# The decayed queries and keys of an HGRN2 level in one tile, scaled and split in one step of 512 columns

## The chip, the cores and the metric

The kernel runs on one core of a Trainium2 chip. The metric is the device time of one execution in microseconds (us). The program is built once; a scheduler in the build decides the order of the instructions on each engine, and on the chip each engine works through its own list in that order, waiting on semaphores where an operand isn't ready. The engines are named PE (TensorE), ACT (ScalarE), DVE (VectorE), POOL (GpSimd) and SP (SyncE, which here issues the weight DMAs).

## The reference

One step of a decoder trunk with two layers, for a prompt of 256 tokens and 8 single sample tokens; the width is 2048. Layer 0 mixes tokens by sliding-window attention and layer 1 by HGRN2, a gated linear recurrence with 12 heads of 128. Both layers have four memory heads, a SiLU gate, one output projection and a LayerNorm. The part that the change touches is the recurrence of the prompt, cut here to what matters:

```python
fg = lb + (1 - lb) * sigmoid(f)          # decay of each token and channel
q, k, v = silu(q), 1 - fg, iv
g_cum = cumsum(log(fg), axis=time)
decay[t, s] = exp(g_cum[t] - g_cum[s])   # s <= t, else 0
scores[t, s] = sum_k q[t, k] * decay[t, s, k] * k[s, k]
o = scores @ v + (q * exp(g_cum)) @ state
o = o * rsqrt(mean(o ** 2) + eps) * norm_w
```

## The kernel before

**The weight stream.** The kernel is a stream of units. A unit is a tile of weights (or of a cache) of 128 x 2048 float32, loaded by the SP queue. `prep` of `Stream` splits it into two float16 parts: the rounded value, hi, on ACT (L97) and the remainder, lo, on DVE (L98); four raw tiles and four split tiles are in flight. The unit's function then multiplies. `passes` (L302 to L305) writes each product as three float16 matmuls: hi by hi (L303), hi by lo (L304), lo by hi (L305). A projection (`proj`, L307) is 16 chunks of three matmuls with 264 columns, 256 prompt tokens and 8 sample tokens.

**Layer 1.** The 12 heads go in six pairs. For each head there are units for the gate f (`f_unit`), the values (`hv_unit`), the queries (`hq_unit`) and the samples' states (`state_unit`). Once the second query of a pair is there, the recurrence of the pair's prompt part is put on as a side (`hg_side`), a generator of which one step runs behind each unit. The last pair's side falls into the time of the memory queries (mq), the samples' memory caches (ck, matmuls mss; cv, matmuls mso) and the gate projections of layer 1 (matmuls g). Behind these come the 16 units of the output projection.

**The side of a pair.** The causal decay is applied level by level, h = 1, 2, 4 up to 64. At a level the tokens form blocks of 2h; the queries of the second half of a block meet the keys of its first half. `qa` (float32) holds the queries times their decay so far, `K`, the prompt's 256 columns of `kk`, the keys. `prepare(h)` splits the first halves of K into `ksp` and the second halves of qa into `qsp` (hi on ACT, L1075, lo on DVE, L1076), and multiplies the same elements by the decays of the level (L1078 for the queries, L1081 for the keys). Each of these steps covers 256 columns: two heads of 128 elements. `products(h)` makes 12 matmuls of 64 columns (hs; stationary ksp, moving qsp) into half of a PSUM bank, and `keep(h)` copies the scores of the level into `st` by a mask on DVE. The four `ksp` buffers are zeroed once, so that the second halves add nothing.

**The end of a side.** `pk` and `kn` turn the decayed keys, `pu` (L1156, float32) multiplies them with the values, `s` and `hpo` (L1167 to L1169) give the outputs, `osb` and `osq` hold the outputs and their squares, `rms` (L1180) sums the squares, and Ln (L1181) and Exp (L1183) make the root of it, for both heads. DVE then scales and gates the result (L1186, L728, L730). The tiles hd, rms, hs and msc (the scores of the memory heads) take turns in two PSUM banks under the tag "sc", so a tile there waits until the second last one before it has been read.

**The order.** Nothing in the source fixes the order between the units and a side's steps beyond the order in which the code is written; the scheduler places the instructions by their dependencies and its own estimates. A change of one tile's shape can therefore move instructions far from it.

Of the kernel before, what the change touches and what calls it, by code (L numbers as in the profile page):

```python
# [35 lines left out]
SA = 8.0  # L36
SP = 1024.0
SK = 2048.0
# [8 lines left out]
LEVELS = (1, 2, 4, 8, 16, 32, 64)  # L47
# [87 lines left out]
def trunk_kernel(  # L135
# [32 lines left out]
    nc = tc.nc  # L168
# [113 lines left out]
    side = deque()  # L282
# [683 lines left out]
    H = {}  # L966

    def open_l1():
        l0.close()
        p1 = l1.enter_context(tc.tile_pool(name="p1", bufs=1))  # L970
        H["p"] = p1
        H["mask"] = p1.tile([P, NMASK], I32, name="mask_t")
        nc.gpsimd.dma_start(H["mask"], mask_d)
        H["sel"] = p1.tile([2 * TS, TS, P], F16, name="sel_t")
        nc.gpsimd.dma_start(H["sel"], sel_d)
        H["ksp"] = [p1.tile([P, 2, 2, TP], F16, name=f"ksp{i}") for i in range(4)]
        for t in H["ksp"]:
            nc.gpsimd.memset(t, 0.0)

    def f_unit(h):  # L980
        def fn(hl):
            if h == 0:
                drain()
                open_l1()
            p1 = H["p"]
            pt = proj(hl, xhl, T, f"f{h}")
            i = h % 2
            if i == 0:
                cur["fg"] = p1.tile([P, 2, T], F32, tag="fg", name=f"fg{h}", bufs=2)
                cur["kk"] = p1.tile([P, 2, T], F32, tag="kk", name=f"kk{h}", bufs=2)  # L990
                cur["ks8"] = p1.tile([P, 2, TS], F32, tag="ks8", name=f"ks8{h}", bufs=2)
            fg, kk, ks8 = cur["fg"][:, i], cur["kk"][:, i], cur["ks8"][:, i]
            th = p1.tile([P, T], F32, tag="th", name=f"th{h}", bufs=2)
            nc.scalar.activation(th, pt, AF.Tanh, scale=0.5 * CP)
            half, mid, half_k, nhalf_k = (hl_lb[:, k, h : h + 1] for k in range(4))
            nc.scalar.activation(fg, th, AF.Identity, bias=mid, scale=half)
            nc.scalar.activation(kk, th, AF.Identity, bias=half_k, scale=nhalf_k)
            nc.vector.tensor_scalar_mul(ks8, kk[:, TP:T], 1.0 / (SA * SK))

        return fn  # L1000

# [2 lines left out]
    def hq_unit(h):  # L1004
        def fn(hl):
            p1 = H["p"]
            pt = proj(hl, xhl, T, f"hq{h}")
            if h % 2 == 0:
                cur["q"] = p1.tile([P, 2, T], F32, tag="hq", name=f"hqs{h}", bufs=2)
            silu2(cur["q"][:, h % 2], pt)  # L1010
            if h % 2 == 1:
                side.append(hg_side(h // 2, cur["q"], cur["vn"], cur["fg"], cur["kk"]))

        return fn

# [35 lines left out]

    osb = {}

    def hg_side(pi, q, vn, fg, kk):
        p1, mask = H["p"], H["mask"]
        h0 = 2 * pi
        K = kk[:, :, :TP]
        Q = q[:, :, :TP]
        st = p1.tile([P, 4, P], F32, tag="st", name=f"st{pi}", bufs=1)
        qa = p1.tile([P, 2, TP], F32, tag="qa", name=f"qa{pi}", bufs=1)  # L1060
# [3 lines left out]
        parts = {}  # L1064

        def prepare(h):
            nonlocal f, off
            n = TP // (2 * h)
            k4 = K.rearrange("p i (n s t) -> p i n s t", s=2, t=h)
            q4 = qa.rearrange("p i (n s t) -> p i n s t", s=2, t=h)  # L1070
            ksp = H["ksp"][LEVELS.index(h) % 4].rearrange("p l i (n s t) -> p l i n s t", s=2, t=h)
            qsp = p1.tile([P, 2, 2, P], F16, tag="qsp", name=f"qsp{pi}_{h}", bufs=4)
            q5 = qsp.rearrange("p l i (n t) -> p l i n t", t=h)
            for hi, lo, src in ((ksp[:, 0, :, :, 0], ksp[:, 1, :, :, 0], k4[:, :, :, 0]), (q5[:, 0], q5[:, 1], q4[:, :, :, 1])):
                nc.scalar.activation(hi, src, AF.Copy)  # L1075
                nc.vector.tensor_tensor(lo, src, hi, op=ALU.subtract)  # L1076
            parts[h] = qsp
            nc.vector.tensor_tensor(  # L1078
                q4[:, :, :, 1], q4[:, :, :, 1], f[:, :, :, 0].unsqueeze(3).to_broadcast([P, 2, n, h]), op=ALU.mult
            )  # L1080
            nc.vector.tensor_tensor(  # L1081
                k4[:, :, :, 0], k4[:, :, :, 0], f[:, :, :, 1].unsqueeze(3).to_broadcast([P, 2, n, h]), op=ALU.mult
            )
            nxt = prod[:, off : off + 2 * n].rearrange("p (i n) -> p i n", i=2)
            if h < 64:
                nc.vector.tensor_tensor(nxt, f[:, :, :, 0], f[:, :, :, 1], op=ALU.mult)
            else:
                nc.vector.scalar_tensor_tensor(nxt, f[:, :, :, 0], 1.0 / SK, f[:, :, :, 1], op0=ALU.mult, op1=ALU.mult)
            off += 2 * n
            if h < 64:  # L1090
                f = nxt.rearrange("p i (n s) -> p i n s", s=2)
            return nxt
# [101 lines left out]
    def state_unit(h):  # L1194
        def fn(hl):
            p1 = H["p"]
            pi, i = h // 2, h % 2
            raw = stream.raw[state_at[h]][:, : TS * P]
            R = raw.rearrange("p (b v) -> p b v", b=TS)
            v = hl[:, :, : TS * P].rearrange("p s (b v) -> p s b v", b=TS)  # L1200
            vr, fgs, ks8 = cur["vr"][:, i], cur["fg"][:, i, TP:T], cur["ks8"][:, i]
            qs, ks, vts = (cur[n][:, i, TP:T] for n in ("q", "kk", "vt"))
# [7 lines left out]
            nc.scalar.activation(qfh[:, :, 0], qf, AF.Copy)  # L1210
# [24 lines left out]
        return fn  # L1235
# [189 lines left out]
```

## Time and profile before

| what | value |
|---|---|
| three runs | 910.62, 910.87, 908.19 us; median 910.62 us |
| the profiled execution: time, span | 909.74 us, 908.0 us |
| mean granted TensorE clock | 0.994 |
| POOL busy | 34.5 us (4%) |
| HBM | 179.80 MB read, 17.22 MB written, 217 GB/s over the span |
| hi of a weight tile, 128x2048, ACT L97 | 1906 ns, 146 of them |
| lo of a weight tile, 128x2048, DVE L98 | 2289 ns, 146 of them |
| a copy of 128x264 on ACT, L997 (kk from th) | 597 ns, 12 of them |
| the six pairs on the time axis | the first hs matmul starts at 465.0 us, the last at 762.9 us |

An engine's busy time is the sum of its instructions' durations. In a timeline, a matmul's row shows its duration with the time in the pipeline; what the engine spends on one is the distance to the next one's start. "Waits" are idle time of an engine in front of an instruction, put down to what ended last before it started. A row of groups gives the line, the engine, the operation, its tiles and shapes, the count, then busy us and mean ns of one, and then the idle time in front of it with its releaser.

### The profile page before, as it was taken

What the parts mean: (1) busy time and instruction counts of PE and PEld (TensorE: products, weight loads), DVE (VectorE), ACT (ScalarE), POOL (GpSimd) and SP (SyncE); (2) the same over time, 40 slices, a digit from 0 to 9 for tenths busy, and PEclk for the clock granted to TensorE, in tenths of its full rate; (3) what the DMA queues carried; (4) which work ended last, traced back from release to release, by engine and by line L of the source; (5) the groups of instructions that cost most, each with busy time, mean ns of one, the idle gap of its engine ahead of it and who ended that gap; (6) DMA issues with size and microseconds to landing.
All of it is one profiled execution on the core that took longest, in us unless ns stands there. A gap on an engine that the chain in (4) does not pass through costs nothing.

```text
span 908.0 us, 21927 instructions
## 1 busy us (share of the span) xinstructions
PE 893.3 (98%) x9281; PEld 764.0 (84%) x9281; DVE 704.2 (78%) x1302; ACT 581.8 (64%) x1000; POOL 34.5 (4%) x65
## 2 busy tenths in 40 slices
PE   9999999999999999999999999999999999899996
PEld 6888889678888888866888888888888888788996
DVE  6879887669886666696697897978888899778736
ACT  6767777567654533576766777676778576948415
POOL 1100010000000000002000000000000000000000
PEclk9999999999999999999999999999999999899999
DMA  9998565567685555555384555726454778566302
GB/s 349 379 369 312 189 242 210 198 210 266 252 318 191 210 204 187 192 203 196 125 310 147 196 183 179 292 100 260 160 208 170 258 267 310 180 251 239 134 1 97
DMA packets 37806, 198.44 MB, mean 219 GB/s; under 512 B 4556, under 2 KB 10733, under 8 KB 17485
## 3 DMA queue, kind: packets, MB, share of 16 engines
q1 hardware_dynamic: 33024, 181.55, 55.4%
q0 software_dynamic: 4640, 15.44, 4.6%
q8 instruction: 72, 1.18, 0.5%
q14 instruction: 26, 0.21, 0.1%
q10 hardware_dynamic: 44, 0.07, 0.1%
HBM read 179.80 MB, written 17.22 MB: 217 GB/s over the span
## 4 chain that ended last, share of the span: by engine, by line
PE 85%; DVE 5%; ACT 4%; DMA 4%; issue 1%; SPq 0%; ACTq 0%; DVEq 0%
PE g L305 6%; PE g L303 6%; PE g L304 6%; PE o L303 5%; PE o L305 5%; PE o L304 5%; PE q L303 2%; PE hv L304 2%; PE hv L303 2%; PE q L304 2%; PE hv L305 2%; PE q L305 2%; PE f L305 2%; PE f L303 2%; PE f L304 2%; ACT hl L97 2%
## 5 line engine op out<-in xcount | busy, mean ns | idle before, releaser
L98 DVE SCALAR_TENSOR_TENSOR hl<-raw,hl 128x2048 f16<-128x2048 f32 (+2 forms) x168 | 358.4, 2137 | 84.4 <-ACT hl L97 83.7
L97 ACT ACTIVATE hl<-raw 128x2048 f16<-128x2048 f32 (+2 forms) x168 | 298.8, 1784 | 87.3 <-PE o L305 45.3
L305 PEld LDWEIGHTS <-hl 128*128 128x128 f16 (+2 forms) x2048 | 197.5, 98 | 32.1 <-DVE hl L98 2.3
L303 PEld LDWEIGHTS <-hl 128*128 128x128 f16 (+2 forms) x2048 | 197.5, 98 | 31.6 <-ACT xhl L249 1.2
L304 PEld LDWEIGHTS <-hl 128*128 128x128 f16 (+2 forms) x2048 | 197.4, 98 | 30.8 <-issue 2.2
L305 PE MATMUL g<-xhl,hl 128*128 128x264 f16 x512 | 142.1, 278 | 1.8 <-DVE hl L98 1.8
L303 PE MATMUL g<-xhl,hl 128*128 128x264 f16 x512 | 142.1, 278 | 0.0
L304 PE MATMUL g<-xhl,hl 128*128 128x264 f16 x512 | 142.1, 278 | 0.0
L303 PE MATMUL o<-mix,hl 128*128 128x264 f16 x384 | 105.5, 276 | 0.7 <-DVE xres L747 0.7
L305 PE MATMUL o<-mix,hl 128*128 128x264 f16 x384 | 105.9, 276 | 0.0
L304 PE MATMUL o<-mix,hl 128*128 128x264 f16 x384 | 105.8, 276 | 0.0
L303 PE MATMUL q<-xhl,hl 128*128 128x264 f16 x192 | 53.0, 276 | 0.5 <-DVE kst L251 0.5
L303 PE MATMUL f<-xhl,hl 128*128 128x264 f16 x192 | 52.9, 276 | 0.4 <-DVE mvhl L251 0.4
L303 PE MATMUL hq<-xhl,hl 128*128 128x264 f16 x192 | 53.1, 276 | 0.0
L304 PE MATMUL hq<-xhl,hl 128*128 128x264 f16 x192 | 53.0, 276 | 0.0
L305 PE MATMUL hq<-xhl,hl 128*128 128x264 f16 x192 | 53.0, 276 | 0.0
L303 PE MATMUL hv<-xhl,hl 128*128 128x264 f16 x192 | 53.0, 276 | 0.0
L304 PE MATMUL hv<-xhl,hl 128*128 128x264 f16 x192 | 53.0, 276 | 0.0
L305 PE MATMUL hv<-xhl,hl 128*128 128x264 f16 x192 | 53.0, 276 | 0.0
L304 PE MATMUL q<-xhl,hl 128*128 128x264 f16 x192 | 53.0, 276 | 0.0
L305 PE MATMUL q<-xhl,hl 128*128 128x264 f16 x192 | 53.0, 276 | 0.0
L305 PE MATMUL f<-xhl,hl 128*128 128x264 f16 x192 | 53.0, 276 | 0.0
(337 smaller groups left out, 1868.4 us busy)
## 6 DMA issues: line engine op xcount, KB each, us to landing
raw<-in_w_in SPq DMA_DIRECT2D x88, 1024.0 KB, 5.5
raw<-in_w_o SPq DMA_DIRECT2D x32, 1024.0 KB, 4.9
raw<-in_w_mk SPq DMA_DIRECT2D x8, 1024.0 KB, 4.9
raw<-in_w_mv SPq DMA_DIRECT2D x8, 1024.0 KB, 4.9
raw<-in_c_mk SPq DMA_DIRECT2D x8, 1024.0 KB, 5.3
raw<-in_c_mv SPq DMA_DIRECT2D x8, 1024.0 KB, 4.8
raw<-in_state SPq DMA_DIRECT2D x12, 512.0 KB, 4.4
out_ss<-raw POOLq DMA_DIRECT2D x12, 512.0 KB, 2.9
```

What stands on the lines that cost most here:

```text
L97: hi = self.nc.scalar.activation(hl[:, 0, s], raw[:, s], AF.Copy, scale=scale)
L98: lo = self.nc.vector.scalar_tensor_tensor(hl[:, 1, s], raw[:, s], scale, hl[:, 0, s], op0=ALU.mult, op1=ALU.subtract)
L303: mm(out, lhs(0), rhs(0), start=start, stop=False)
L304: mm(out, lhs(0), rhs(1), start=False, stop=False)
L305: return mm(out, lhs(1), rhs(0), start=False, stop=stop)
```

## The change

The float32 queries `qa` and keys `K` become the two halves of one tile `qk32`, 128 x 2 (q, k) x 2 heads x 256. `f_unit` writes the prompt's keys into it, and the sample tokens' keys, 8 columns, into a `kk` of their own by an ACT instruction of its own. The four `ksp` tiles and the rotating `qsp` tiles become four tiles with hi and lo of both. `halves_of(t, h)` describes, in one access pattern, the queries' second halves and the keys' first halves of a level. `prepare(h)` makes one hi copy, one lo subtraction and one multiplication of 512 columns, where each was two of 256. The moving operand of hs is read in place, in runs of h elements with gaps of h, where qsp had it without gaps. Only the keys' half of the float16 tiles is zeroed.

```diff
-        H["ksp"] = [p1.tile([P, 2, 2, TP], F16, name=f"ksp{i}") for i in range(4)]
-        for t in H["ksp"]:
-            nc.gpsimd.memset(t, 0.0)
+        H["qk"] = [p1.tile([P, 2, 2, 2, TP], F16, name=f"qk16_{i}") for i in range(4)]
+        for t in H["qk"]:
+            nc.gpsimd.memset(t[:, :, 1], 0.0)
...
+                cur["qk"] = p1.tile([P, 2, 2, TP], F32, tag="qk32", name=f"qk32_{h}", bufs=2)
+                cur["kk"] = p1.tile([P, 2, TS], F32, tag="kk", name=f"kk{h}", bufs=2)
...
-            nc.scalar.activation(kk, th, AF.Identity, bias=half_k, scale=nhalf_k)
-            nc.vector.tensor_scalar_mul(ks8, kk[:, TP:T], 1.0 / (SA * SK))
+            nc.scalar.activation(cur["qk"][:, 1, i], th[:, :TP], AF.Identity, bias=half_k, scale=nhalf_k)
+            nc.scalar.activation(kk, th[:, TP:T], AF.Identity, bias=half_k, scale=nhalf_k)
+            nc.vector.tensor_scalar_mul(ks8, kk, 1.0 / (SA * SK))
...
+    def halves_of(t, h):
+        a, n = t[:, 0, 0, h : h + 1], TP // (2 * h)
+        inner = [[TP, 2], [2, n]] if h == 1 else [[2 * h, 2 * n], [1, h]]
+        return bass.AP(tensor=a.tensor, offset=a.offset, ap=[list(a.ap[0]), [2 * TP - h, 2], *inner])
...
-            for hi, lo, src in ((ksp[:, 0, :, :, 0], ksp[:, 1, :, :, 0], k4[:, :, :, 0]), (q5[:, 0], q5[:, 1], q4[:, :, :, 1])):
-                nc.scalar.activation(hi, src, AF.Copy)
-                nc.vector.tensor_tensor(lo, src, hi, op=ALU.subtract)
-            parts[h] = qsp
-            nc.vector.tensor_tensor(
-                q4[:, :, :, 1], q4[:, :, :, 1], f[:, :, :, 0].unsqueeze(3).to_broadcast([P, 2, n, h]), op=ALU.mult
-            )
-            nc.vector.tensor_tensor(
-                k4[:, :, :, 0], k4[:, :, :, 0], f[:, :, :, 1].unsqueeze(3).to_broadcast([P, 2, n, h]), op=ALU.mult
-            )
+            src = halves_of(qk, h)
+            hi, lo = (halves_of(H["qk"][LEVELS.index(h) % 4][:, s], h) for s in range(2))
+            nc.scalar.activation(hi, src, AF.Copy)
+            nc.vector.tensor_tensor(lo, src, hi, op=ALU.subtract)
+            by = f.rearrange("p i n s -> p s i n")
+            if h > 1:
+                by = by.rearrange("p s i n -> p s (i n)").unsqueeze(3).to_broadcast([P, 2, 2 * n, h])
+            nc.vector.tensor_tensor(src, src, by, op=ALU.mult)
...
         def products(h, sc):
-            qsp, ksp = parts.pop(h), H["ksp"][LEVELS.index(h) % 4]
+            t = H["qk"][LEVELS.index(h) % 4]
+            q5 = t[:, :, 0].rearrange("p l i (c n s t) -> p l i c n s t", c=2, s=2, t=h)
...
-                    lambda s: ksp[:, s, i, c * P : (c + 1) * P],
-                    lambda s: qsp[:, s, i, c * 64 : (c + 1) * 64],
+                    lambda s: t[:, s, 1, i, c * P : (c + 1) * P],
+                    lambda s: q5[:, s, i, c, :, 1],
```

In the built programs DVE has 1102 rows where it had 1190, ACT 772 where it had 796; PE has as many instructions as before, and SP issues the same DMAs in the same order. ACT's table loads are 20 where they were 16. In the changed program the lines of the RMS block stand one line higher (Ln at L1180, Exp at L1182, rms at L1179). The scheduler gives other places to many instructions; the following three are those of the last two pairs. Numbers behind names tell buffers apart.

The first place is ACT in the RMS block of the fifth pair, among the memory queries. Before (osq: the squares; rms: their sums; qsp and ksp: splits of the last pair's first levels; hl: hi of a weight tile):

```order
L97 ACTIVATE hl_10199<-raw_10035 128x2048
L1181 ACT_TABLE_LOAD
L1181 ACTIVATE osq_10047<-rms_10107,eps_rms 128x264
L1075 ACTIVATE qsp_1_10182<-qa_10174 128x256
L1181 ACTIVATE osq_10049<-rms_10110,eps_rms 128x264
L1183 ACT_TABLE_LOAD
L1183 ACTIVATE osq_10047<-osq_10047 128x264
L1183 ACTIVATE osq_10049<-osq_10049 128x264
L1075 ACTIVATE qsp_2_10191<-qa_10174 128x256
```

The same place in the changed program (qk_1: the split of both at the second level):

```order
L97 ACTIVATE hl_10150<-raw_9910 128x2048
L1180 ACT_TABLE_LOAD
L1180 ACTIVATE osq_9920<-rms_9980,eps_rms 128x264
L1182 ACT_TABLE_LOAD
L1182 ACTIVATE osq_9920<-osq_9920 128x264
L1180 ACT_TABLE_LOAD
L1180 ACTIVATE osq_9922<-rms_9983,eps_rms 128x264
L1182 ACT_TABLE_LOAD
L1182 ACTIVATE osq_9922<-osq_9922 128x264
L1076 ACTIVATE qk_1_5654<-qk_10_9343 128x2x128x2
```

The first head's Exp has moved ahead of the second head's Ln, with a table load on each side of it. On PE, the 12 hs of the last pair's first level now stand directly behind its hd, where 13 matmuls of mq stood between them.

The second place is ACT in the RMS block of the last pair. Before (sil: a gate's SiLU; msphl: the split of the samples' memory probabilities):

```order
L1171 ACTIVATE osb_9827<-hpo_10750 128x2x256
L1175 ACTIVATE osq_10758<-osb_9827 128x264
L1175 ACTIVATE osq_10760<-osb_9827 128x264
L97 ACTIVATE hl_10959<-raw_10693 128x2048
L733 ACTIVATE sil_11013<-g_10964 128x264
L249 ACTIVATE msphl_10815<-mback_10812 128x64
L1181 ACT_TABLE_LOAD
L1181 ACTIVATE osq_10758<-rms_10818,eps_rms 128x264
L1181 ACTIVATE osq_10760<-rms_10821,eps_rms 128x264
L1183 ACT_TABLE_LOAD
L1183 ACTIVATE osq_10758<-osq_10758 128x264
L1183 ACTIVATE osq_10760<-osq_10760 128x264
```

And in the changed program:

```order
L1170 ACTIVATE osb_9700<-hpo_10594 128x2x256
L1174 ACTIVATE osq_10602<-osb_9700 128x264
L1174 ACTIVATE osq_10604<-osb_9700 128x264
L1180 ACT_TABLE_LOAD
L1180 ACTIVATE osq_10602<-rms_10662,eps_rms 128x264
L1182 ACT_TABLE_LOAD
L1182 ACTIVATE osq_10602<-osq_10602 128x264
L1180 ACT_TABLE_LOAD
L1180 ACTIVATE osq_10604<-rms_10665,eps_rms 128x264
L249 ACTIVATE msphl_10659<-mback_10656 128x64
L1182 ACT_TABLE_LOAD
L1182 ACTIVATE osq_10604<-osq_10604 128x264
```

Here too the first Exp has moved ahead of the second Ln; and the hi of a weight tile and a SiLU that stood between the squares and the first Ln have moved to ahead of `s` and behind the block.

The third place is PE at the end of the last pair. Before, this is how the block around rms began (g: a gate projection; mback: the samples' probabilities, turned back):

```order
L677 MATMUL mback_10812<-ident,mrows_10804 128x32 x2
L305 LDWEIGHTS hl_10905
L305 MATMUL g_11094<-xhl,hl_10905 128x264
L303 LDWEIGHTS hl_10905
L303 MATMUL g_11094<-xhl,hl_10905 128x264
L304 LDWEIGHTS hl_10905
L304 MATMUL g_11094<-xhl,hl_10905 128x264
L1180 MATMUL rms_10818<-osq_10758,ones_rms 128x264
```

In the changed program the block from pu to the first msc reads:

```order
L1155 MATMUL pu_10523<-vn_9499,kn_10484 128x128 x4
L666 MATMUL mrow_10645<-ident,mst_10643 32x128 x2
L1168 MATMUL hpo_10594<-qk_10_9343,s_10528 128x128
L1166 MATMUL hpo_10594<-st_10046,vn_9499 128x128
L1167 MATMUL hpo_10594<-st_10046,vn_9499 128x128
L1168 MATMUL hpo_10594<-qk_10_9343,s_10528 128x128
L1179 MATMUL rms_10662<-osq_10602,ones_rms 128x264
L1179 MATMUL rms_10665<-osq_10604,ones_rms 128x264
L677 MATMUL mback_10656<-ident,mrows_10648 128x32 x2
L303 LDWEIGHTS mqhl
L303 MATMUL msc_10732<-mkhl,mqhl 128x256
```

Before, 80 matmuls of two gate projections (32 of g_10964 and 48 of g_11094) stood between pu and the last mso. Now all matmuls of the gate projections that are ready stand ahead of pu, two of hpo stand there as well, and between pu and the next gate projection PE has only the pair's own chain, msc, mso and mpt.

More of the change, by code (lines that the diff above doesn't have):

```diff
@@ L989, in fn @@
                 cur["fg"] = p1.tile([P, 2, T], F32, tag="fg", name=f"fg{h}", bufs=2)
-                cur["kk"] = p1.tile([P, 2, T], F32, tag="kk", name=f"kk{h}", bufs=2)
+                cur["qk"] = p1.tile([P, 2, 2, TP], F32, tag="qk32", name=f"qk32_{h}", bufs=2)
+                cur["kk"] = p1.tile([P, 2, TS], F32, tag="kk", name=f"kk{h}", bufs=2)
                 cur["ks8"] = p1.tile([P, 2, TS], F32, tag="ks8", name=f"ks8{h}", bufs=2)
@@ L1011, in fn @@
             if h % 2 == 1:
-                side.append(hg_side(h // 2, cur["q"], cur["vn"], cur["fg"], cur["kk"]))
+                side.append(hg_side(h // 2, cur["q"], cur["vn"], cur["fg"], cur["qk"]))
         return fn
@@ L1052, in trunk_kernel, with hg_side @@
     osb = {}
-    def hg_side(pi, q, vn, fg, kk):
+    def halves_of(t, h):
+        a, n = t[:, 0, 0, h : h + 1], TP // (2 * h)
+        inner = [[TP, 2], [2, n]] if h == 1 else [[2 * h, 2 * n], [1, h]]
+        return bass.AP(tensor=a.tensor, offset=a.offset, ap=[list(a.ap[0]), [2 * TP - h, 2], *inner])
+    def hg_side(pi, q, vn, fg, qk):
         p1, mask = H["p"], H["mask"]
         h0 = 2 * pi
-        K = kk[:, :, :TP]
+        qa, K = qk[:, 0], qk[:, 1]
         Q = q[:, :, :TP]
         st = p1.tile([P, 4, P], F32, tag="st", name=f"st{pi}", bufs=1)
-        qa = p1.tile([P, 2, TP], F32, tag="qa", name=f"qa{pi}", bufs=1)
         prod = p1.tile([P, 2 * TP], F32, tag="prod", name=f"prod{pi}", bufs=1)
@@ L1063, in hg_side @@
         off = 0
-        parts = {}
         def prepare(h):
@@ L1068, in prepare @@
             n = TP // (2 * h)
[L1069 to L1073, printed above, removed]
-            for hi, lo, src in ((ksp[:, 0, :, :, 0], ksp[:, 1, :, :, 0], k4[:, :, :, 0]), (q5[:, 0], q5[:, 1], q4[:, :, :, 1])):
-                nc.scalar.activation(hi, src, AF.Copy)
-                nc.vector.tensor_tensor(lo, src, hi, op=ALU.subtract)
-            parts[h] = qsp
-            nc.vector.tensor_tensor(
-                q4[:, :, :, 1], q4[:, :, :, 1], f[:, :, :, 0].unsqueeze(3).to_broadcast([P, 2, n, h]), op=ALU.mult
-            )
-            nc.vector.tensor_tensor(
-                k4[:, :, :, 0], k4[:, :, :, 0], f[:, :, :, 1].unsqueeze(3).to_broadcast([P, 2, n, h]), op=ALU.mult
-            )
+            src = halves_of(qk, h)
[6 more added lines that the diff above has]
+            nc.vector.tensor_tensor(src, src, by, op=ALU.mult)
             nxt = prod[:, off : off + 2 * n].rearrange("p (i n) -> p i n", i=2)
@@ L1201, in fn @@
             vr, fgs, ks8 = cur["vr"][:, i], cur["fg"][:, i, TP:T], cur["ks8"][:, i]
-            qs, ks, vts = (cur[n][:, i, TP:T] for n in ("q", "kk", "vt"))
+            qs, vts = (cur[n][:, i, TP:T] for n in ("q", "vt"))
+            ks = cur["kk"][:, i]
             if i == 0:
```

## The prediction

> **What bounds the kernel now.** The page comes first: the busy line, the slices, the chain.
>
> ```profile
> PE 893.3 (98%) x9281; PEld 764.0 (84%) x9281; DVE 704.2 (78%) x1302; ACT 581.8 (64%) x1000; POOL 34.5 (4%) x65
> PE   9999999999999999999999999999999999899996
> PEclk9999999999999999999999999999999999899999
> PE 85%; DVE 5%; ACT 4%; DMA 4%; issue 1%; SPq 0%; ACTq 0%; DVEq 0%
> ```
>
> TensorE (PE) is busy 98% of the span, and it carries 85% of the chain that ended last. VectorE (DVE) and ScalarE (ACT) have slack as a whole, so a saving there is worth only what PE waits for them. One slice dips in PE and in the granted clock, slice 35 of 40 (about 772 to 794 us): the tail of the last HGRN2 pair. PE's waits over the run, and the stages by windows, show the same.
>
> ```profile
> PE g L305 <- DVE hl L98: 1.8, 1, 1.8
> PE msc L303 <- ACT ms L614: 0.7, 1, 0.7
> PE mso L696 <- ACT hl L97: 0.5, 1, 0.5
> PE hs L303 <- ACT qsp L1075: 0.5, 3, 0.2
> ```
>
> ```profile
> 512.00:566.00 54.00, 53.84 (x565) 47.12 (x564) 45.27 (x99) 38.87 (x73) 1.61 (x3) 1.00 0.54 195
> 784.50:787.90 3.40, 2.95 (x27) 2.16 (x27) 3.36 (x7) 3.40 (x9) 0.00 (x0) 0.50 0.21 36
> 787.90:791.30 3.40, 1.70 (x32) 1.43 (x29) 3.40 (x7) 3.40 (x2) 0.00 (x0) 1.00 0.67 272
> 791.30:794.80 3.50, 3.42 (x16) 2.39 (x17) 3.50 (x5) 3.50 (x9) 0.00 (x0) 0.51 0.66 218
> ```
>
> (The waits give us in total, times, longest; the windows give start:end, length, then busy us of PE, weight load, DVE, ACT and POOL, clock, DMA share, GB/s.) From 512 to 566, a whole pair of heads, PE misses 0.16 of 54 us. All of the work that the change edits costs PE 0.5 us in the run: three waits of hs for the query split. The tail is different: there ACT is busy 3.40 of 3.40 us and PE waits 0.5, 0.7 and 1.8 us, 3.0 in sum; and twice the clock is granted at half (0.50 and 0.51), costing about 1.7 us each, since 3.4 us at half clock do 1.7 us of work. So two questions decide: does the wide form reach PE at all, and what does the new order do near a place where ACT is already late?
>
> **The wide steps.** Per pair and level there were two hi copies on ACT, and on DVE two lo subtractions and two multiplications, of 256 columns; now there is one of each, of 512.
>
> ```profile
> L1075 ACT ACTIVATE qsp<-qa 128x256 f16<-128x256 f32 x42 | 17.5, 417 | 20.3 <-DVE qa L1078 16.6 <-DVE qa L1119 3.5
> L1076 DVE TENSOR_TENSOR qsp<-qa,qsp 128x256 f16<-128x256 f32 x42 | 17.6, 419 | 1.5 <-ACT qsp L1075 1.5
> L1078 DVE TENSOR_TENSOR qa<-qa,prod 128x256 f32<-128x256 f32 x36 | 15.0, 417 | 0.1
> L1119 DVE SCALAR_TENSOR_TENSOR qa<-hqs,fg 128x512 f32<-128x512 f32 x6 | 4.1, 683 | 0.0
> L1171 ACT ACTIVATE osb<-hpo 128x512 f32<-128x512 f32 x6 | 3.5, 582 | 2.7 <-PE hpo L1169 2.7
> L1210 ACT ACTIVATE qfh<-qf 128x8 f16<-128x8 f32 x12 | 2.5, 205 | 0.0
> ```
>
> DVE: 42 levels × (4 × 418 − 2 × 683 ns) = 12.9 us less by durations (a 512-column step priced by L1119). ACT: 42 × (2 × 417 − 582) = 10.6 us less; the 12 new copies of 8 columns add 12 × 0.205 = 2.5 us. Nearly all of this lies beside PE, by the 512:566 row. What reaches PE is at most the 0.5 us of hs. Against it, the K half of a level could be split early and now waits for qa; at level 1 one wide hi and lo follow qa in place of narrow ones, (582 − 417) + (683 − 419) = 0.43 us later, but at level 2 two copies fewer stand in the way. If PE's cover failed six times this would be 6 × 0.43 = +2.6 us. I take **−0.5 us**, bounds −0.5 and +2.6, nearer to the row of the waits. POOL's smaller memsets and the unchanged SP queue count as nothing: POOL is 4% busy.
>
> **The loads between Ln and Exp.** The order of the changed kernel moves the RMS block of the last two pairs from Ln, Ln, Exp, Exp to Ln, Exp, Ln, Exp. Each change of function carries a table load.
>
> ```profile
> L1181 ACT ACT_TABLE_LOAD x6 | 7.7, 1283 | 0.1
> L1183 ACT ACT_TABLE_LOAD x6 | 7.7, 1283 | 0.1
> ```
>
> Six pairs had two loads each; now two of them have four, so 4 × 1.283 = 5.1 us of ACT come back, and at those two places PE has little beside it. The Trainium skill, "ScalarE: Activation LUTs", section "Table sets: the hidden batching unit", says that Ln followed by Exp needs a single load, as one set holds both. By that nothing would be added and the sum would be the cover rival's below; the two rows above disagree, with a load in front of each. The same page, section "What ACT_TABLE_LOAD costs", adds a drain of about 1380 ns to each load; in the rows below the Ln starts 1.29 us after its load starts, so the drain isn't seen. With it, three extra loads on the path would make the sum about 4 us longer.
>
> *The fifth pair (queries of the memory heads).*
>
> ```profile
> 725.70 0.61 PE L1180 MATMUL rms<-osq,ones_rms 128*128 128x264 f32 x2
> 726.64 1.28 ACT L1181 ACT_TABLE_LOAD   x1
> 729.06 1.05 PE L1118 MATMUL hd<-hqs,kk 128*128 128x128 f32 x8
> ```
>
> hs of level 1 needs the PSUM bank of the second rms, which the second Ln frees. Before, that Ln came right behind the first, and 13 mq matmuls stood between hd and hs. Now two loads and an Exp stand ahead of it, and hs follows hd directly. From the start of the first rms, PE passes two rms, 21 mq and hd: 2 × 0.44 + 21 × 0.1125 + 0.9 ≈ 4.15 us (0.44 for an rms: in the timeline the second starts 0.55 behind the first with one mq of 0.11 between; 0.1125 from the g rows below; hd's row is 1.05 with the tail of its last pass). ACT starts its load 0.5 to 0.94 us behind that rms (0.94 in the row: 726.64 − 725.70) and needs load 1.30, Ln 0.4, load 1.30, Exp 0.37, load 1.30, Ln 0.45, 5.1 in sum, so it ends at 5.6 to 6.0. PE waits 1.4 to 1.9 us: **+1.5 us**. Bounds: 0, if the arrival is later than counted, and +3.5, if half a clock window (1.7) follows, as at 784.5.
>
> *The last pair.* Before, PE filled the chain pu, hpo, square, rms, Ln, Exp, msc, mso with 80 gate matmuls; in the changed order they all stand ahead of pu.
>
> ```profile
> 766.99 1.05 PE L1156 MATMUL pu<-vn,kn 128*128 128x128 f32 x8
> 779.75 0.28 PE L304 MATMUL g<-xhl,hl 128*128 128x264 f16 x1
> 780.20 0.28 PE L305 MATMUL g<-xhl,hl 128*128 128x264 f16 x1
> 791.38 0.40 PE L305 MATMUL g<-xhl,hl 128*128 128x264 f16 x1 [1.78 <-DVE hl L98]
> ```
>
> ```profile
> 768.08 0.38 ACT L1160 ACTIVATE s<-pu 128x256 f32<-128x256 f32 x1
> 771.61 0.46 ACT L672 ACTIVATE mrows<-mrow,mrnm 32x256 f32<-32x256 f32 x1 [3.14 <-DVE mrnm L671]
> 772.08 0.57 ACT L1171 ACTIVATE osb<-hpo 128x512 f32<-128x512 f32 x1
> 772.68 0.74 ACT L1175 ACTIVATE osq<-osb 128x264 f32<-128x264 f32 x2
> 775.64 1.28 ACT L1181 ACT_TABLE_LOAD   x1
> 776.93 0.85 ACT L1181 ACTIVATE osq<-rms,eps_rms 128x264 f32<-128x264 f32 x2
> 779.10 0.73 ACT L1183 ACTIVATE osq<-osq 128x264 f32<-128x264 f32 x2
> 780.83 0.42 ACT L729 ACTIVATE mix<-sil 128x264 f16<-128x264 f32 x1 [1.00 <-DVE sil L728]
> 783.89 0.46 ACT L614 ACTIVATE ms<-msc,mnm 128x256 f32<-128x256 f32 x1
> 787.76 3.72 ACT L97 ACTIVATE hl<-raw 128x2048 f16<-128x2048 f32 x2
> 789.04 2.28 DVE L98 SCALAR_TENSOR_TENSOR hl<-raw,hl 128x2048 f16<-128x2048 f32 x1
> ```
>
> From pu to the gate matmul that waits for DVE's hl it was 791.38 − 766.99 = 24.4 us. 80 gates of 0.1125 us (0.45 us for four, 779.75 to 780.20) are 9.0 us; two hpo matmuls that now precede pu are 0.45 (half of pu's row less its last pass's tail), and eight msc (256 columns against the gates' 264, so 0.109 each, 0.87) now stand behind: 10.3 us of work leaves this stretch, and is done elsewhere. With no new loss the stretch would be 14.1 us. In the new order I follow ACT from pu's start: s by 1.5; mrows by 2.6, once DVE's reduction is there; osb 0.57 and the two squares 0.74, by 4.0; then load, Ln, load, Exp, load, Ln, msphl (0.2, by the 8-column row), load, Exp, that is 4 × 1.28 + 2 × 0.43 + 2 × 0.37 + 0.2 = 6.9: 10.9. msc of the second half needs the second Ln's bank, at 9.1; mso comes at 9.85. Then DVE scales and gates, three steps of about 0.45 (264 columns, by L1076's 419 ns for 256): 12.3; ACT: mix 0.42, a SiLU 0.4 by that row, and two ms of 0.46, to 13.9; the hi copy 1.9 (3.72 for two): 15.8; DVE's lo 2.28: **18.1**. So the stretch is 18.1 − 14.1 = **4.0 us** longer, which I round up by the semaphores' steps to +4.1. The half clock that followed the last wait (791.30 row) is in both. Bounds: 0, if cover is found, and +7.8, where the hi copy that now stands on ACT ahead of s (1.9) delays it all, and one more half-clock window (1.7) comes with the longer wait.
>
> **Sum**: 909.74 (this execution; span 908.0) − 0.5 + 1.5 + 4.1 = **914.8 us**. The median of the three runs shown, 910.62, is 0.1% above the profiled time.
>
> **The rivals.**
> - *Faster.* ACT and DVE are the engines that PE waits for in the tail, and they lose 8 and 13 us of work. If that pulls the hi and lo of the gate weights forward, the 3.0 us of waits there and the 0.5 at hs go: 909.74 − 3.5 = 906.2. It decides if the tail's ACT work shrinks; but the saved copies lie before 766, and in the tail itself the order adds two loads. Chance 0.10.
> - *Cover.* The narrow steps were free and so are the loads, because PE still has gates queued there: 909.74 − 0.5 = 909.2. For it, the 512:566 row; against it, the order behind pu, without a gate. Also the case in which the change cuts instructions and nothing else. Chance 0.24.
> - *Strided queries.* The moving operand of hs is now read in runs of h elements with gaps of h, where it was contiguous.
>
> ```profile
> 523.58 0.19 PE L305 MATMUL hs<-qsp,ksp 128*128 128x64 f16 x1
> 523.84 0.19 PE L305 MATMUL hs<-qsp,ksp 128*128 128x64 f16 x1
> ```
>
> Nine steps in 0.26 us are 29 ns each. The kernel has 504 of them; at twice the time that is +14.6 us on top: 929. It decides from about 6 ns each (3 us). No strided moving operand of this kind is in the trace; bounds 0 and +14.6, and I take 0, as 64 columns in 29 ns are what the shape needs. The Trainium skill, "Advanced Engine Details and Errata", section "SBUF Cachelines", asks for at least two hits on a 16-byte line; a gap of one f16 leaves four, so by it this rival falls away and the sum stays; no run shows it yet. Chance 0.08.
>
> **How the numbers follow.** The forecast has 0.58, with a range of its own from 912 to 919.5 (bounds of the three terms, not all at their ends together). A measurement of this kernel can tell about 0.3% from no change: 907.0 to 912.5. Of the 0.58 I give 0.04 to lie below 912.5. So faster 0.10, within 0.3% 0.24 + 0.04 = 0.28, slower 0.54 + 0.08 = 0.62. The range from 908.5 to 919.5 holds the forecast and the cover case, 0.82; faster and strided are left out.
>
> **What would show it.** Right: in the profile after, four loads at each of the last two RMS blocks; a wait of 1 to 2 us of hs for the second Ln; between pu and the next gate matmul a stretch near 18 us with some 8 us of PE idle; the 512:566 kind of stage unchanged; hs still every 29 ns. Wrong: loads, yet no PE wait behind them (cover), hs slower than 35 ns (strided), or the gate weights split before PE asks (faster). A wait in the steady pairs for the wide lo of level 1 would break the first term.

## The result: 920.09 us, slower by 1.1%

| kernel | runs | median (range) us | ratio to the kernel before, 95% interval |
|---|---|---|---|
| before | 4 | 909.68 (908.19 to 910.87) | |
| changed | 4 | 920.09 (919.08 to 923.05) | 1.0112 (1.0089 to 1.0136) |
| changed, measured again (e9) | 4 | 918.83 (918.05 to 920.10) | 1.0095 (1.0081 to 1.0109) |

The direction was the forecast one, but the loss is 8.5 to 10.4 us, where 5.1 was forecast, and the first median lies 0.6 us above the range. The page of the changed kernel (the execution of 919.61 us, span 917.8), its busy line, two rows of slices and the chain:

```profile
PE 897.6 (98%) x9281; PEld 765.1 (83%) x9281; DVE 702.1 (76%) x1218; ACT 587.7 (64%) x974; POOL 34.6 (4%) x65
PE   9999999999999999999999999999999989799996
PEclk9999999999999999999999999999999999699998
PE 82%; DVE 6%; DMA 5%; ACT 4%; issue 2%; SPq 0%; ACTq 0%; DVEq 0%
```

One instruction of DVE in fifteen is gone (1218 where the page before has 1302: two fewer at each of the 42 levels; the rows of the built programs differ by 88, for which no profile shows a reason), and the kernel is slower: PE is still what sets the time. Its slices dip in one more place than before (slice 33, about 734 to 757 us), and the dip at slice 35 is deeper, with the clock at 0.6. The longest waits of PE in layer 1 name what it waited for (us in total, times, longest):

```profile
PE msc L303 <- ACT osq L1180: 2.1, 1, 2.1
PE hs L303 <- ACT osq L1180: 1.4, 1, 1.4
PE hs L303 <- ACT qk L1076: 1.2, 2, 0.8
PE hpo L1168 <- ACT s L1159: 1.2, 1, 1.2
PE rms L1179 <- ACT osq L1174: 1.1, 1, 1.1
PE msc L303 <- DVE sil L734: 1.0, 1, 1.0
PE g L305 <- DVE hl L98: 0.8, 2, 0.6
```

All of these stand in the last two pairs. Where the time went is read most simply from the starts of the same matmul in the timelines of both kernels:

| matmul | before, us | changed | changed again | lost since the row above |
|---|---|---|---|---|
| the first f, layer 1 begins | 418.99 | 420.57 | 419.13 | 1.58 and 0.14 |
| an hv late in the fifth pair | 692.33 | 693.81 | 692.38 | -0.10 and -0.09 |
| the 1261st gate matmul, behind the memory queries | 753.64 | 757.55 | 756.11 | 2.43 and 2.42 |
| an o of the last projection | 833.64 | 843.85 | 842.65 | 6.30 and 6.54 |

The first row is no effect of the change: up to there no instruction of any engine stands elsewhere in the order. Over the thirteen profiled executions of this study whose layer 0 is the same program, this start lies between 418.64 and 423.36 us. What the change does is in the last two rows, 8.7 to 9.0 us together in both profiles. Ahead of the first, second and fourth matmul of the table the same matmuls have run in both kernels; ahead of the third, 13 hs fewer in the changed one, 0.4 us of PE's work. With these counted where they belong, 2.8 us are lost at the memory queries and 5.9 to 6.2 us in the tail.

*The memory queries.* ACT's timeline, then the first and the last hs of the last pair's level 1 from PE's (start, duration, and in brackets the idle time before it with what ended it):

```profile
733.45 1.28 ACT L1180 ACT_TABLE_LOAD   x1
734.75 0.48 ACT L1180 ACTIVATE osq<-rms,eps_rms 128x264 f32<-128x264 f32 x1
735.25 1.28 ACT L1182 ACT_TABLE_LOAD   x1
736.54 0.43 ACT L1182 ACTIVATE osq<-osq 128x264 f32<-128x264 f32 x1
736.99 1.28 ACT L1180 ACT_TABLE_LOAD   x1
738.28 0.48 ACT L1180 ACTIVATE osq<-rms,eps_rms 128x264 f32<-128x264 f32 x1
738.78 1.28 ACT L1182 ACT_TABLE_LOAD   x1
```

```profile
738.81 0.19 PE L303 MATMUL hs<-qk 128*128 128x64 f16 x1 [1.44 <-ACT osq L1180]
739.14 0.19 PE L305 MATMUL hs<-qk 128*128 128x64 f16 x1
```

Two loads stand between the two Ln, and hs starts when the second ends, 1.44 us late. The two Ln start 3.5 us apart, of which 0.48 us is the Ln. The two hs rows are 11 steps apart in 0.33 us: 30 ns each, with the strided queries.

*The tail.* PE, ACT and DVE from pu to the gate matmul that needs DVE's lo:

```profile
781.32 1.05 PE L1155 MATMUL pu<-vn,kn 128*128 128x128 f32 x8
783.76 0.49 PE L1168 MATMUL hpo<-qk,s 128*128 128x128 f32 x2 [1.16 <-ACT s L1159]
801.13 0.40 PE L305 MATMUL g<-xhl,hl 128*128 128x264 f16 x1 [0.20 <-DVE hl L98]
```

```profile
781.52 1.91 ACT L97 ACTIVATE hl<-raw 128x2048 f16<-128x2048 f32 x1 [2.33 <-PE g L305]
783.34 0.37 ACT L1159 ACTIVATE s<-pu 128x256 f32<-128x256 f32 x1
791.16 0.48 ACT L1180 ACTIVATE osq<-rms,eps_rms 128x264 f32<-128x264 f32 x1
793.08 0.42 ACT L1182 ACTIVATE osq<-osq 128x264 f32<-128x264 f32 x1
796.54 3.71 ACT L97 ACTIVATE hl<-raw 128x2048 f16<-128x2048 f32 x2
```

```profile
798.79 2.28 DVE L98 SCALAR_TENSOR_TENSOR hl<-raw,hl 128x2048 f16<-128x2048 f32 x1
```

The stretch takes 801.13 - 781.32 = 19.8 us. The windows of the tail give PE, weight load, DVE, ACT and POOL busy, the granted clock, DMA's share and GB/s:

```profile
773.00:776.00 3.00, 2.38 (x30) 1.87 (x29) 2.80 (x3) 1.67 (x2) 0.00 (x0) 1.00 0.80 325
781.30:786.60 5.30, 2.99 (x22) 2.45 (x21) 3.65 (x7) 4.22 (x8) 0.03 (x1) 1.00 0.33 138
786.60:803.30 16.70, 13.26 (x169) 9.45 (x168) 10.21 (x21) 15.41 (x24) 0.51 (x1) 0.50 0.26 85
```

PE runs dry already at 773 to 776 (a wait of 0.6 us for a gate's lo at 775.25, as all of the gate's matmuls are now called for ahead of pu), is idle for 2.3 of the first 5.3 us behind pu, and then the clock stays at half for 16.7 us. ACT works 15.4 of these 16.7 us: with DVE, which takes over from it for the gating and the last lo, it is the bound of the tail.

### The profile page after: what moved, and what is told of

It is laid out like the page before. It is cut to its first block, busy times and chain, and to the rows that moved or that the text cites. A ratio compares the mean times of both kernels' runs of the same rounds, so it can differ in the third digit from the quotient of the medians.

```text
span 917.8 us, 21788 instructions
## 1 busy us (share of the span) xinstructions
PE 897.6 (98%) x9281; PEld 765.1 (83%) x9281; DVE 702.1 (76%) x1218; ACT 587.7 (64%) x974; POOL 34.6 (4%) x65
## 4 chain that ended last, share of the span: by engine, by line
PE 82%; DVE 6%; DMA 5%; ACT 4%; issue 2%; SPq 0%; ACTq 0%; DVEq 0%
PE g L303 5%; PE g L305 5%; PE o L303 5%; PE g L304 5%; PE o L305 5%; PE o L304 5%; DVE hl L98 3%; PE hq L303 2%; PE hq L305 2%; PE f L303 2%; PE f L304 2%; PE hq L304 2%; PE f L305 2%; PE hv L305 2%; PE hv L303 2%; PE hv L304 2%
```

## The experiments

Three theories stood against each other. ORDER: what costs is where the scheduler put the matmuls, Ln and Exp. LOADS: the four added table loads are all of it. WIDE: the steps of 512 columns come late by themselves. Each run is compared with runs of the kernel before on the same chip.

| run | kernel | median us | ratio (95% interval) | layer 1 on, by the profiles' starts, us |
|---|---|---|---|---|
| | changed, twice | 920.09, 918.83 | 1.0112, 1.0095 | +8.3, +8.8 |
| e1 | changed, Exp behind both Ln | 914.35 | 1.0045 (1.0028 to 1.0062) | +4.0 |
| e2 | before, Ln and Exp interleaved | 915.35 | 1.0056 (1.0035 to 1.0077) | +3.4 |
| e3 | e1, two gates behind pu | 923.49 | 1.0147 (1.0123 to 1.0170) | +13.3 |
| e4 | changed, two gates behind pu | 925.48 | 1.0167 (1.0144 to 1.0189) | +14.8 |
| e5 | wide, PE's old order throughout | 914.81 | 1.0054 (1.0034 to 1.0075) | +4.1 |
| e6 | narrow, PE's new order | 925.97 | 1.0179 (1.0159 to 1.0198) | +13.8 |
| e7 | e5 with one table for Ln and Exp | 920.52 | 1.0118 (1.0101 to 1.0134) | +11.9 |
| e8 | wide, old order from the fifth pair | 914.17 | 1.0042 (1.0026 to 1.0058) | +2.7 |
| e10 | wide, old order from the first pk | 908.49 | 0.9977 (0.9959 to 0.9994) | -2.7 |
| e11 | e1, old order from the fifth rms | 913.40 | 1.0036 (1.0020 to 1.0051) | +4.5 |

The last column is the start of a late matmul of the output projection against that in the kernel before (877.42 us), less the same difference at the first f. It is one profile each, and a median and its profile can differ by 2 us.

**The loads, taken out and put in.** e1 orders each pair's Exp behind both Ln; PE's order at the queries stays, and no gate stands behind pu:

```diff
-            nc.scalar.activation(sq, pm[:, :T], AF.Ln, bias=eps_rms)
+            ln = nc.scalar.activation(sq, pm[:, :T], AF.Ln, bias=eps_rms)
         for i, sq in enumerate(sqs):
-            nc.scalar.activation(sq, sq, AF.Exp, scale=-0.5)
+            with tc.issue_after(ln.ins):
+                nc.scalar.activation(sq, sq, AF.Exp, scale=-0.5)
```

> The changed kernel, with each pair's first Exp queued behind its second Ln on ACT; 16 table loads in place of 20, PE's order in the queries' stage as in the changed kernel, and still no gate matmul between pu and mso. Theory ORDER (the loss is two places: the interleaved loads at the memory queries, and the last pair's chain without gates beside it): the waits of hs (1.4 + 1.2 us) go and two loads of the last chain (about 2.6 us) go, so about 5 us faster than the changed kernel, 914 to 916 us, with hpo, rms and msc in the last chain still waiting. Theory LOADS (the four added loads are all of it): 909 to 911 us. Theory WIDE (the steps of 512 columns come late by themselves): less than 1 us of gain, 919 to 920 us.

914.35 us: ORDER's figure, and 4.5 to 5.7 us less than the changed kernel. In PE's waits, 0.3 us of hs is all that is left at the queries:

```profile
PE g L305 <- DVE hl L98: 2.4, 2, 1.7
PE mso L696 <- DVE msphl L251: 1.3, 1, 1.3
PE hpo L1168 <- ACT s L1159: 1.2, 1, 1.2
PE rms L1179 <- ACT osq L1174: 1.1, 1, 1.1
PE hs L303 <- ACT qk L1076: 0.3, 1, 0.3
```

hpo and rms behind pu wait as they did, and mso and the gates behind them wait too. By the starts, all that e1 loses is lost behind the 1261st gate matmul. So the interleaved loads are about half of the loss, and the tail in its new order the rest, some 4 us. e2 puts the loads into the last two pairs of the kernel before, with the second Ln queued behind the first Exp:

```diff
+        apart = ExitStack()
...
+            with apart:
+                nc.scalar.activation(sq, pm[:, :T], AF.Ln, bias=eps_rms)
+            if pi > 3:
+                ex = nc.scalar.activation(sq, sq, AF.Exp, scale=-0.5)
+                apart.enter_context(tc.issue_after(ex.ins))
```

> The kernel before with Ln, Exp, Ln, Exp in the last two pairs, by edges on ACT's order alone: 20 table loads, narrow steps, and the 13 mq matmuls between hd and hs and the gates behind pu where they were. Theory ORDER: the gates and the mq matmuls cover the most of it, so +0 to +3 us, 910 to 913 us; if PE waits anywhere, it is at msc or mso of the last pair. Theory LOADS: +8 to +10 us, 918 to 920 us, with the table loads alone. Theory WIDE: no change, 909 to 910.5 us.

915.35 us, +5.1: above ORDER's 910 to 913, below LOADS' 918. I had taken the gates and the mq matmuls for cover, and they cover little:

```profile
PE hs L303 <- ACT ksp L1075: 1.9, 1, 1.9
PE msc L303 <- ACT osq L1183: 1.7, 1, 1.7
PE mso L696 <- ACT hl L97: 1.4, 1, 1.4
```

PE waits not only for the Ln, but for what stands behind the loads on ACT: the keys' hi at the queries, a weight tile's hi in the tail. Taken out or put in, the interleaving is worth about 5 us by the medians; by its one profile, the fastest of its six runs, e2 loses 3.4.

**The gates behind pu, by hand.** e3 and e4 queue the gates 12 and 13, 96 matmuls, behind the last pu; e3 has e1's edit too.

```diff
-            pt = proj(hl, xhl, T, f"g{l}{j}")
+            with tc.issue_after(cur["pu"].ins) if l and j in (12, 13) else nullcontext():
+                pt = proj(hl, xhl, T, f"g{l}{j}")
```

> The changed kernel with both repairs: Exp behind both Ln, and the matmuls of two gate projections (12 and 13) queued behind the last pu on PE, so that 96 gate matmuls lie beside the last chain. Theory ORDER: all of the loss goes, 908 to 911 us, and PE's waits between pu and mso shrink below 2 us. Theory LOADS: the same as with the Exps moved alone. Theory WIDE: 918 to 920 us.

> The changed kernel with the gate matmuls queued behind the last pu, without an order for Exp. The order on ACT becomes Ln, Ln, Exp, Exp in the last pair by itself and stays interleaved at the memory queries. Theory ORDER: the tail's 5 to 6 us go, the hs waits (1.4 + 1.2 us) stay: 911.5 to 914 us. Theory LOADS: half of the loss goes with two loads: 914 to 916 us. Theory WIDE: 918 to 920 us.

Both miss on the wrong side, 923.49 and 925.48 us. PE's waits of e3:

```profile
PE mpt L622 <- DVE ms L617: 4.1, 1, 4.1
PE hs L304 <- DVE qk L1078: 2.3, 1, 2.3
PE hs L303 <- ACT qk L1077: 1.6, 2, 1.2
PE pk L1150 <- DVE qk L1082: 1.0, 1, 1.0
```

The waits of hpo, rms and msc behind pu are gone, but mpt, which stands behind pu and behind the gates put there, waits 4.1 us at 806.7, the longest wait of the run; and ahead of pu the hs and pk of the last pair and pu itself now wait, bare of the gates that lay beside them. In the kernel before, 16 of the 96 matmuls stood ahead of pu and the rest in seven places between pu and the last mso. So neither "few gates behind pu" nor "more gates behind pu" is the rule. That the cover has to be spread over the whole chain, as it is in the kernel before, fits, but isn't tested by these two runs, and they say nothing on WIDE.

**The two orders, exchanged whole.** Both kernels have the same 9155 matmuls, written in the same sequence by the program. So one kernel can be given the other's order on PE: a table of runs (first number and length; that of e10 is shown, cut), and an edge of issue order from each matmul to the next.

```diff
+ORDER = (
+    "4739+6 4760+20 4727+1 4780+4 4745+1 4784+14 4832+2 4728+11 4798+2 4834+23 4826+1 4800+1 4827+4 4801+25 "
...
+    order = [a for r in ORDER.split() for a in range(int(r.split("+")[0]), sum(map(int, r.split("+"))))]
+    for a, b in zip(order, order[1:]):
+        tc.add_manual_dep(mms[b], mms[a].name, edge, reason="order")
```

The table shifts the lines of these kernels by up to 31. e5, e8, e10 and e11 differ in where the chain begins, and e11 has e1's edit as well. With the old matmul order, the scheduler puts Ln, Ln, Exp, Exp on ACT by itself in e5, e8 and e10, with 16 loads.

> The changed kernel with all its matmuls chained, by edges of issue order, in exactly the order that they have on PE in the kernel before; ACT and DVE are placed by the scheduler around it (Ln, Ln, Exp, Exp and 16 table loads come out of that). Theory ORDER (only the order of the matmuls and of Ln and Exp costs, the wide steps nothing): 908.5 to 911 us, the waits of PE as before (3.0 us in the tail). Theory WIDE (steps of 512 columns come late where PE asks early): PE waits at hs for hi or lo of the wide splits, several us in all, 913 us or more. If the saved instructions of DVE and ACT are worth something, it ends below 908.5.

> The kernel before, narrow steps, with its matmuls chained in the order that they have on PE in the changed kernel. On ACT the fifth pair's Ln and Exp are interleaved by the scheduler (18 table loads), the last pair's are Ln, Ln, Exp, Exp. Theory ORDER: it loses as the changed kernel does with one pair's loads fewer, 915 to 919 us, with hs waiting for the second Ln at the memory queries and hpo, rms and mso in the last chain. Theory WIDE: 909 to 912 us.

e5's 914.81 us fit WIDE by the number and ORDER by the place. From the starts, it has lost 7.0 us between the first f and the end of the second pair's side (575 us), and gains on the kernel before from there on (-0.6 up to the tail, -2.3 in it). One wait does it, and the half clock behind it:

```profile
PE pk L1176 <- DVE qk L1108: 4.4, 1, 4.4
```

```profile
493.00:498.00 5.00, 0.60 (x14) 0.39 (x12) 4.35 (x5) 1.41 (x2) 0.00 (x0) 0.85 0.41 144
498.00:502.00 4.00, 4.00 (x19) 3.11 (x20) 0.00 (x0) 0.87 (x2) 0.00 (x0) 0.50 0.61 244
```

It is the first pair alone, in which the chain begins, some 27 us ahead of this wait; there DVE has a weight tile's lo (494.23, 2.28 us) ahead of the level-64 split. Pairs two to six, chained alike, have no such wait. e6, the narrow steps in PE's new order, is the other exchange: 925.97 us, so the narrow steps lose by this order at least as much as the wide ones (by the starts 13.8 against 8.3 to 8.8; ACT and DVE were ordered anew by the scheduler there too, so the 5 us between is not the worth of the wide steps alone). WIDE predicted 909 to 912.

Three more starts of the chain, to tell the seam from the steps:

> The changed kernel with the matmuls chained in the order of the kernel before only from the fifth pair's level 16 on (the last 1227 places in which the two orders differ); the first four pairs keep the changed kernel's own order. In the version chained throughout, one wait of 4.4 us at the first pair's pk and the half clock behind it took 7.0 us, and everything behind it came 2.9 us nearer to the kernel before. Theory ORDER: without that wait 907 to 910 us, no wait of hs at the memory queries, the tail's waits below 3 us. Theory WIDE: PE waits at hs, pk or st of the last pair, 913 us or more.

> The changed kernel with the matmuls in the order of the kernel before from the first pair's pk on; up to there the changed kernel's own order. The chained versions so far lost 5 to 7 us at the place where the chain begins (pk of the first pair; hs of the fifth), where hi and lo of a weight tile stand ahead of the level's split on ACT and DVE. If that is a cost of the place of the seam and not of the wide steps, this version ends at 907 to 911 us with one short wait at most near the first pk; if wide steps are late whenever PE keeps the old order, the wait of 4 us at pk returns, 914 us or more.

> The changed kernel with the first Exp behind the second Ln, and the matmuls chained in the order of the kernel before only from the fifth pair's rms on, so through the memory queries and the tail. Theory ORDER: 907 to 911 us, the tail as in the kernel before (mso 0.5, msc 0.7, g 0.8 to 1.8 us). If the seam costs here too, a wait of hs or hd of the last pair of 2 us or more, 912 to 915 us.

e8 (914.17 us) again loses at the beginning of its chain: 4.8 us at hs of levels 16 and 32 and the matmuls behind them; behind that it gains 2 us in the tail. e11 (913.40 us) loses 4.8 us at the fifth pair's hpo and rms, where its chain begins. e10 begins at the first pk, and there the place is quiet:

```profile
PE g L329 <- DVE hl L122: 1.5, 1, 1.5
PE msc L327 <- ACT ms L638: 0.7, 1, 0.7
PE mso L720 <- ACT hl L121: 0.5, 1, 0.5
PE pk L1173 <- DVE qk L1105: 0.2, 1, 0.2
```

The waits of the tail are those of the kernel before but for a shorter one of g (1.5 us where it was 1.8; 0.7 and 0.5 as before), hs waits nowhere, and the time is 908.49 us, below the kernel before by 0.23% (0.06 to 0.41). It is the best of this study: the wide steps with the matmuls in the old order from the first pk on. So in that order the wide steps do not lose, and the kernel is about 2 us faster. That e8 and e11 lose by the place at which two orders are joined fits with this quiet seam. For e5 it is less sure: its wait stands well behind the beginning of its chain, in the first pair, whose hs e10 leaves in the new order; that the wide steps come late there, in that one pair, isn't excluded.

What the 2 us are made of is another matter. By the starts, in one profile of each, e10 is 0.6 us ahead at the 1261st gate matmul and 2.7 us at the o of the last projection. Of the 2.1 us between, 0.3 is the shorter wait of g and 1.6 is the clock: behind that wait the kernel before ran at 0.51 (791.3 to 794.8), and e10 at 1.00:

```profile
792.00:796.00 4.00, 3.82 (x34) 3.34 (x35) 4.00 (x6) 4.00 (x8) 0.00 (x0) 1.00 0.68 242
```

e11 has the same order of the matmuls there, but its clock is at 0.50 behind the wait (795.6 to 800.6), and it gains nothing in the tail. So most of the 2 us hang on whether a stretch of half clock falls behind the last wait, and that the saved work keeps it away isn't shown.

**One table for Ln and Exp.** e7 adds to e5, for the last two pairs, a load of the set that holds both, behind the squares, and queues the SiLU of gate 12 behind the Exp:

```diff
+        if pi > 3:
+            with tc.issue_after(squared.ins):
+                nc.scalar.preload_act_table_set("natural_log_exp_and_others")
```

> As the wide steps in the old order, and for the last two pairs the table set that holds both Ln and Exp is loaded ahead of them, behind the squares, with the SiLU of gate 12 queued behind the last Exp: no load between Ln and Exp, and the first load lies in time in which ACT waits for rms. Theory ORDER with loads on the chain of the tail: the Exp of the last pair comes 1.3 to 2.6 us earlier, and of the 6.4 us that the tail loses some 1 to 3 go: 906.5 to 909 us. If the tail is bound by the hi and lo of the gate weights alone: no change against the version without it.

A miss: 920.52 us, 5.7 more than e5. No load stands between Ln and Exp of the last two pairs, but PE gets new waits at hs (2.4 us), msc (2.8 us) and mpt (2.2 us), as the scheduler moved other work of ACT and DVE around the edit. The worth of the single load by itself stays open.

**The changed kernel again.**

> The changed kernel itself once more, for its interval and a second profile. If the 1.6 us that its profile lost in layer 0, where no instruction differs, is scatter of executions, the second profile loses another amount there (between -0.2 and 1.6 us), and the same waits stand at the memory queries (hs 1.4 + 1.2 us) and in the tail within 0.3 us; the median stays between 917 and 922 us.

918.83 us. hs waits 1.4 + 1.2 us as before, hpo 1.2, rms 1.1; msc's longest wait for Ln is 2.7 where it was 2.1, more than the 0.3 us that I had allowed, and layer 0 lost 0.14 us instead of 1.58. So the places hold, and 1.4 us between the two profiles is scatter of layer 0.

## Why the prediction fell short, point by point

- **What bounds the kernel**: right. The rows of waits name only the last two pairs, and from the first f to the fifth pair the wide steps moved PE by -0.1 us.
- **The wide steps, -0.5 us**: the three waits at hs went, but it is -0.1 by the starts: up to the hv of the table the hs take 0.8 us less by their spacing, and the other matmuls, in their new order, 0.7 us more. The prices were near for DVE, low for ACT:

```profile
L1076 ACT ACTIVATE qk<-qk 128x512 f16<-128x512 f32 x42 | 27.5, 654 | 27.9 <-DVE qk L1081 24.2 <-DVE qk L1118 3.5 <-DVE qf L1208 0.2
L1077 DVE TENSOR_TENSOR qk<-qk,qk 128x512 f16<-128x512 f32 x42 | 29.2, 695 | 11.8 <-ACT qk L1076 11.7
L999 ACT ACTIVATE kk<-th,hl_lb 128x8 f32<-128x8 f32 x12 | 4.6, 384 | 0.0
```

  695 ns stand against 683, 654 against 582, and the copy of 8 columns takes 384 where the nearest row had 205. None of it reached PE.
- **The queries, +1.5 us**: the named wait came as named, 1.44 us of hs for the second Ln. Missed are the next two: hs of levels 4 and 8 wait 0.8 and 0.45 us for their hi, the one behind a weight tile's hi on ACT (742.59, 1.89 us), the other behind its multiplication on DVE. By the starts the stage lost 2.8 us. The step that failed: the working stopped at the first matmul that a late Ln frees, and didn't follow ACT's queue to the next level; e1, without the loads, has 0.3 us there.
- **The last pair, +4.1 us**: the mechanism is right and the term too small, 5.9 to 6.2 us. The stretch from pu to the gate's lo was put at 18.1 us and takes 19.8. The step that failed is "s by 1.5": the hi of a weight tile that the order shows ahead of s (781.52, 1.91 us) starts after pu does, and s ends 2.4 us behind pu's start. The delay grows on the way: the squares end at 5.0 where 4.0 was worked out, the last Exp at 12.2 for 10.9, the hi begins at 15.2 for 13.9. That hi ahead of s stood among the bounds (+1.9), and not in the sum, though the order had it there for certain. The rest lies ahead of pu, where PE caught up with DVE at a gate's lo (0.8 us at 774, by the spacing of the matmuls), and was not looked for. PE is idle for 5.7 us of the stretch, where some 8 were expected: its matmuls took longer, at half clock. That the half clock itself cost little more than before is an estimate: up to 801.13 what came last was ACT's or DVE's work, and from there to 803.3 it held back some 1.1 us of PE's.
- **The sum**: -0.1 + 2.8 + 6.0 = 8.7 us, against the 8.5 to 10.4 of the medians; the 9.87 us between the two profiles first compared hold 1.58 us of layer 0. The upper bounds of the three terms added up to 923.6; the range was cut at 919.5 with the argument that they would not all come together, and two of the three came out well above their figures. Two small slips of the working, 13.9 for 14.0 and +7.8 for +7.7, play no part.
- **The rivals**: cover, 0.24, falls: loads in the kernel before cost 5.1 us beside all of its gates (e2). Faster falls as a result of this change; with the order kept the kernel is about 2 us faster (e10), but 1.6 of these are the clock in the tail, and not hi and lo that came earlier. Strided falls: 30 ns for an hs against 29.
- **The page on tables.** The Trainium skill ("ScalarE: Activation LUTs", "Table sets: the hidden batching unit") counts one load for Ln followed by Exp. In these programs that holds only where the common set is loaded explicitly, as in e7; else each of the two brings its own, and the changed kernel's 8 and 8 loads in the RMS blocks follow the order on ACT.

That the order and not the steps is the cause is shown by e10 (the same steps, old order from the first pk on: no loss) and e6 (old steps, new order of the matmuls: a loss, with ACT and DVE placed anew as well). The half at the loads is shown by e1 and e2. The half in the tail is shown by its place in e1; that it is the missing gates that cost there is argued from the waits, and putting gates back by hand did not mend it (e3, e4). Why the scheduler chose the new order is open.

## What to carry to other kernels

Where a scheduler places the work, compare the orders that it makes before judging an edit by the instructions that it saves: here 84 fewer instructions on DVE came with about 2 us, most of them by the clock, and the order that came with them cost 10 to 12 (918.83 and 920.09 against e10's 908.49). Price a moved wait with everything that the built order puts ahead of it on the engine that ends it, and follow that engine's queue on to the next things that PE asks for. When a version loses by its order, fix the order at the places that wait, and mind where the fixed part begins.

## What the hardware showed that I had not expected

- Saved busy time of narrow instructions is much less than their durations. In the timeline of the kernel before, DVE's instructions overlap:

```profile
520.85 0.42 DVE L1081 TENSOR_TENSOR kk<-kk,fg 128x256 f32<-128x256 f32 x1
521.18 0.68 DVE L1121 SCALAR_TENSOR_TENSOR st<-hd,ident 128x512 f32<-128x512 f32 x1
521.79 0.42 DVE L1076 TENSOR_TENSOR qsp<-qa,qsp 128x256 f16<-128x256 f32 x1
```

  A step of 256 columns lasts 0.42 us, and the next starts after 0.33; of 512, 0.68 and 0.61. Four narrow ones take 1.32 us, two wide ones 1.22, so a level saves about 0.1 us of DVE, by these starts, and not the 0.3 that the durations say. The section on time and profile calls an engine's busy time the sum of its instructions' durations; the page in fact counts time in which two of them overlap once. DVE's durations add up to 782.9 us before and 772.5 after, its busy times are 704.2 and 702.1: 2.1 us less, and not the 12.9 worked out.
- The clock stayed at half for 16.7 us with PE's single waits no longer than 2.1 us and PE busy 13.3 of the 16.7. Several short waits in a row were followed by a longer stretch at half clock than e5's one wait of 4.4 us, behind which the clock was at 0.50 from 498 to 502. The Trainium skill ("TensorE: Matmul & The Clock Gate", "HAM oscillation — how this bites in real kernels") puts the rule as no idle gap of PE over some 3.4 us; here the clock fell without such a gap.
